# Four gate rows sent through DRAM instead of the matrix engine, and a written order for the last in-products

## The chip, the cores and the metric

The program runs on one core of a Trainium2 chip. The metric is the device time of one execution in microseconds. The core has a matrix engine (TensorE, PE in the profile; PEld is its weight load, which overlaps the matmuls), three engines for elementwise work (VectorE = DVE, ScalarE = ACT, GpSimd = POOL) and a queue of DMAs that SyncE (SP) issues. On-chip memory is SBUF, with 128 partitions; matmuls write to PSUM, whose banks the kernel gives out from two pools.

## What is computed

A two-layer diffusion backbone over 512 latent tokens and 256 context tokens of width 1024. The first layer mixes tokens by pooling, the second by attention; each is followed by a squared-ReLU MLP of width 4096. Six rows of 1024 numbers for each layer, made from a conditioning vector, shift, scale and gate the sub-layers:

```python
for i in range(DEPTH):
    sh1, sc1, gt1, sh2, sc2, gt2 = ada_mods(c, w_ada[i], b_ada[i])
    csh1, csc1, cgt1, csh2, csc2, cgt2 = ada_mods(c_ctx, w_ada[i], b_ada[i])
    ...
    x = x + gt1 * rms_norm(y_lat, g_mix_post[i])
    m_lat = sq_relu_mlp(modulate(rms_norm(x, g_mlp_pre[i]), sh2, sc2), w_mlp_in[i], w_mlp_out[i])
    x = x + gt2 * rms_norm(m_lat, g_mlp_post[i])
    if not last:
        ...
        ctx = ctx + cgt2 * rms_norm(m_ctx, g_mlp_post[i])
```

The change is about the gates (gt1, gt2, cgt2): rows of 1024 numbers by which every token's row is multiplied, so that on the chip each of the 128 partitions, one for a token, wants a copy of the whole row.

## The kernel before, in words

Activations and weights are 32-bit. A product of two of them is made from three matmuls of rounded parts: each operand is split into a high part (cast on ACT, POOL) and a low part (the difference, mostly on DVE).

**Stages.** Pooling mixer; first MLP over all 768 tokens in six rows of 128 (0 to 3 latent, 4 and 5 context); projection to q, k and v; attention; output projection; second MLP over the four latent rows; output. Each MLP runs over sixteen groups of 256 hidden columns.

**First MLP.** The hidden columns of one group are seven in-products over half the tokens each (class `Seven`, chains 0 to 6, in a Strassen-like scheme; tiles psin in PSUM), combined by ACT and DVE into the hidden rows, which are squared and split into high and low (rb). Then each of the six token rows takes twelve matmuls for each half of its 1024 columns (tiles pso, `out_mm`), which are added to acc (`out_ev`). The last two groups are done together in `finish`: each row takes 24 pso matmuls a half, ordered so that the ones that need only the older group come first. `finish` goes through the rows in the order 4, 5, 0, 1, 2, 3. Rows 4 and 5 are added to acc by DVE; the others start from a copy of acc in PSUM (ACT, pso<-acc).

**After a row.** ACT squares and sums it (junk, ss), POOL or DVE makes the inverse root rs, DVE multiplies the row by the gate (work<-acc,gate or work<-pso,gate) and adds it, scaled, to the residual (xr or xl). Normed rows are transposed by PE (psx<-ident,acc), modulated by ACT and DVE (acc<-psx) and split (ra), as operands of the projection (psq). The tiles pso, psx's neighbours psg, psq and psy share a pool of four PSUM banks (psB): a new one can only start when the row product of an old one has read it.

**Gates before.** `gate_cols` makes a gate as eight columns of 128 (tile gc), one value to a partition. To repeat it over partitions there are two ways. `gate_rows` lets PE multiply a broadcast column by the identity, eight matmuls (in the program; each shows as two in the trace) of 128x128, and ACT copies the two halves from PSUM. `gate_diag` splits gc into high and low (gh), lets DVE make two diagonal tiles of 128x1024 (diag), sums them with two matmuls a half by a matrix of ones (psg<-diag,onesr), and again ACT copies. Before the change, the two GT2 gates of layer 0 are made by `gate_diag` in `before0`, which is called between the last in-products and `finish(0)`; the GT2 gate of layer 1 by `gate_diag` within `finish(1)`; the GT1 gate of layer 1 by `gate_rows` near the end of attention. Tile gate holds two rows (ci 0 for latent, 1 for context tokens).

**What sets the order.** Python code hands operations over in the order of written times (`Steps`, `at(time, function)`), which is their priority; a scheduler that simulates engines then sets each engine's order from it. Within an engine, instructions run in that order. Some are pinned to the program's order (`pin`), and some get a manual dependency (`tc.add_manual_dep(.., ISSUE)`), which only orders them on their own engine, without a semaphore. DMAs stand in SP's order; one that waits holds those behind it.

## Time and profile before

| what | value |
|---|---|
| median of three runs | 1156.81 us (1156.76 to 1157.1) |
| the profiled execution | 1157.33 us |
| its span in the profile | 1155.2 us, clock 0.999 |
| PE busy | 1134.3 us (98%) |
| PEld, DVE, ACT, POOL busy | 979.8, 938.0, 644.8, 74.4 us |
| chain that ended last | PE 94%, DMA 3%, ACT 2%, DVE 1% |
| psg<-diag matmuls | 12, 3.7 us |
| psg<-ident matmuls | 48, 6.2 us (16 of them at the end of attention) |
| diag products on DVE | 6, 7.2 us |
| gate<-psg copies on ACT | 12, 6.6 us |

The span runs from the first to the last instruction of the profiled execution; the execution's own time has about 2 us around it. A row of the trace gives a start and a length in us from the span's start; matmuls are pipelined, so that neighbouring rows overlap a little, and twelve matmuls of 128x512 take about 2.75 us from one start to the next.

### The profile page before, as it was taken

Reading aid. Unit: us, or ns where it says so; the run is one execution under the profiler, and the core shown is the slowest. Engines: PE = TensorE matmul, PEld = TensorE weight load, DVE = VectorE, ACT = ScalarE, POOL = GpSimd, SP = SyncE. Lnnn points to the kernel's source line nnn. Section 1 sums busy time; section 2 is a strip of 40 time slices with the busy share of each in tenths; the row PEclk is TensorE's granted clock in tenths of the full one; section 3 lists DMA queues with packets and bytes.
Section 4 is the critical chain, followed back from the end, with each engine's and each line's share of the span. In section 5 each row is a group of like instructions: output and inputs, shape, how many; then the busy total and the mean of one; then the engine's idle time right before and its main releaser. Section 6 shows DMA issues by size and latency. Waiting matters only on the chain.

```text
span 1155.2 us, 15680 instructions
## 1 busy us (share of the span) xinstructions
PE 1134.3 (98%) x6026; PEld 979.8 (85%) x6026; DVE 938.0 (81%) x1551; ACT 644.8 (56%) x1150; POOL 74.4 (6%) x82
## 2 busy tenths in 40 slices
PE   6999999999999999999999999999999999999998
PEld 5579889998899988998888889988988888888886
DVE  5798488889989898998778698978887779778876
ACT  6476655555435434555786378863876436534524
POOL 3040000000000000000231312100000000000000
PEclk9999999999999999999999999999999999999999
DMA  9992233244434444344442200145244224314303
GB/s 355 398 390 99 74 109 110 80 140 146 146 109 146 146 147 146 109 146 146 187 142 99 84 1 20 34 134 208 82 146 146 79 68 146 109 40 144 109 28 118
DMA packets 95305, 152.08 MB, mean 132 GB/s; under 512 B 2896, under 2 KB 68224, under 8 KB 95232
## 3 DMA queue, kind: packets, MB, share of 16 engines
q1 hardware_dynamic: 95136, 151.07, 37.8%
q8 instruction: 47, 0.77, 0.3%
q14 instruction: 26, 0.21, 0.1%
q10 hardware_dynamic: 96, 0.02, 0.0%
HBM read 141.65 MB, written 9.44 MB: 131 GB/s over the span
## 4 chain that ended last, share of the span: by engine, by line
PE 94%; DMA 3%; ACT 2%; DVE 1%; issue 0%; POOL 0%; DVEq 0%; SPq 0%; ACTq 0%
PE pso L68 36%; PE psin L68 35%; PE psq L68 7%; PE psy L68 4%; PE po L68 3%; PE pss L68 3%; DMA raw<-in_w_ada 2%; PE pspt L68 1%; PE psada L68 1%; PE pspool L68 1%; PE psx L68 1%; PE psg L68 1%; ACT ra L68 0%; DMA xr<-in_ctx 0%; DMA gate<-in_band 0%; ACT xr L68 0%
## 5 line engine op out<-in xcount | busy, mean ns | idle before, releaser
L68 PE MATMUL pso<-units,rb 128*128 128x512 f32 x1152 | 277.3, 392 | 0.0
L68 PEld LDWEIGHTS pso<-units,rb 128*128 128x128 f32 x1152 | 214.9, 188 | 41.7
L68 DVE TENSOR_TENSOR acc<-acc,pso 128x512 f32<-128x512 f32 x192 | 128.3, 680 | 61.5 <-PE pso L68 61.4
L68 DVE SCALAR_TENSOR_TENSOR rows<-raw,cond,rows 128x256 f32<-128x256 f32 x280 | 123.4, 483 | 0.9
L68 PE MATMUL psin<-ra 128*128 128x512 f32 (+1 forms) x424 | 112.4, 369 | 0.6 <-ACT work L68 0.6
L68 PE MATMUL psin<-ra,rb 128*128 128x512 f32 (+1 forms) x384 | 101.6, 360 | 0.0
L68 DVE TENSOR_TENSOR units<-raw,units 128x1024 fp32r<-128x1024 f32 (+2 forms) x69 | 82.4, 1203 | 13.8 <-ACT units L68 13.7
L68 ACT CAST units<-raw 128x1024 fp32r<-128x1024 f32 (+2 forms) x71 | 70.7, 1019 | 41.0 <-PE pso L68 21.8
L68 PE MATMUL psin<-rb,ra 128*128 128x384 f32 (+1 forms) x324 | 90.6, 356 | 0.0
L68 PEld LDWEIGHTS psin<-ra 128*128 128x128 f32 x424 | 77.8, 188 | 12.3 <-ACT work L68 1.0
L68 ACT ACTIVATE work<-psin 128x512 f32<-128x512 f32 (+3 forms) x66 | 36.0, 551 | 84.6 <-PE psin L68 82.4
L68 PE MATMUL psin<-ra,units 128*128 128x384 f32 x432 | 82.6, 336 | 0.4 <-ACT psin L68 0.4
L68 PE MATMUL pso<-units,pairs 128*128 128x512 f32 x336 | 82.3, 389 | 0.0
L68 PEld LDWEIGHTS psin<-ra,units 128*128 128x128 f32 x432 | 76.4, 188 | 3.2 <-ACT psin L68 0.5
L68 PEld LDWEIGHTS psin<-ra,rb 128*128 128x128 f32 x384 | 66.7, 189 | 11.5 <-issue 0.8
L68 PEld LDWEIGHTS pso<-units,pairs 128*128 128x128 f32 x336 | 63.1, 188 | 13.1
L68 PE MATMUL psin<-sums,units 128*128 128x384 f32 x336 | 63.6, 336 | 0.0
L68 PEld LDWEIGHTS psin<-rb,ra 128*128 128x128 f32 x324 | 58.6, 188 | 5.5
L68 ACT COPY acc<-pso 128x512 f32<-128x512 f32 x68 | 38.5, 592 | 40.1 <-PE pso L68 39.9
L68 PEld LDWEIGHTS psin<-sums,units 128*128 128x128 f32 x336 | 59.0, 188 | 1.3
L68 ACT CAST rb<-raw 128x2048 fp32r<-128x2048 f32 (+2 forms) x18 | 25.8, 1431 | 58.3 <-PE pso L68 55.8
L68 ACT ACTIVATE work<-work 128x768 f32<-128x768 f32 (+1 forms) x50 | 41.4, 831 | 28.8 <-DVE work L68 28.3
(226 smaller groups left out, 2118.9 us busy)
## 6 DMA issues: line engine op xcount, KB each, us to landing
raw<-in_w_ada SPq DMA_DIRECT2D x48, 1024.0 KB, 5.4
raw<-in_w_mlp_in SPq DMA_DIRECT2D x32, 1024.0 KB, 5.3
raw<-in_w_mlp_out SPq DMA_DIRECT2D x32, 1024.0 KB, 6.0
raw<-in_w_qkv SPq DMA_DIRECT2D x6, 1024.0 KB, 5.1
spill<-xl SPq DMA_DIRECT2D x8, 512.0 KB, 5.5
xl<-spill SPq DMA_DIRECT2D x8, 512.0 KB, 7.1
raw<-in_w_o SPq DMA_DIRECT2D x4, 1024.0 KB, 5.0
xl<-in_x SPq DMA_DIRECT2D x4, 512.0 KB, 5.5
```

Source lines behind the costliest of these rows:

```text
L68: z = made(*args, **kw)
```

## The change

A tensor grows of four rows is added in DRAM. `gate_away` makes the columns gc and stores them there as one row of 1024 numbers (a DMA of 128 x 8 single elements on SP's queue); `gate_back` loads that row into gate for all 128 partitions (one DMA, 512 KB written). The three `gate_diag` calls and the one `gate_rows` call go. The stores of layer 0's GT2 gates are called in groups 7 and 8 of the first MLP, that of layer 1's GT1 in `before0` (the scheduler moves it up to the middle of the first MLP, as its columns are ready there), and that of layer 1's GT2 in the second MLP; the loads are called where the gates were made before, ahead of the loads of the residual. On SP the stores stand between loads of weights (two between the loads that were issued at 291.79 and 304.17 before), the first two loads directly ahead of xr<-spill and xl<-spill.

Beside that, in `finish(0)` the matmuls of the first two rows (4 and 5) get manual dependencies: of row 4, matmuls n = 0 and 1 of each half are free, n = 2 and 3 come behind the last matmul of chain 4, and the rest of row 4 and all of row 5 behind chain 6.

```diff
--- before.py
+++ after.py
@@ -113,6 +113,7 @@
     psA = ctx.enter_context(tc.tile_pool(name="psA", bufs=2, space=PSUM))
     psB = ctx.enter_context(tc.tile_pool(name="psB", bufs=4, space=PSUM))
     spill = ctx.enter_context(tc.tile_pool(name="spill", bufs=1, space=bass.MemoryType.DRAM)).tile([P, NT, D], F32, name="spill")
+    rows_out = ctx.enter_context(tc.tile_pool(name="grows", bufs=1, space=bass.MemoryType.DRAM)).tile([4, D], F32, name="grows")
 
     acc = const.tile([P, NT * D], F32, name="acc")
     ident = const.tile([P, P], F32, name="ident")
@@ -379,6 +380,16 @@
                               start=True, stop=True)
                 pin(z, i == 0 and m == GT1)
             sc.copy(gate[:, ci, 512 * h:512 * h + 512], ps)
+
+    row_of = {(0, GT2, 0): 0, (0, GT2, 1): 1, (1, GT1, 0): 2, (1, GT2, 0): 3}
+
+    def gate_away(i, m, ci):
+        gc = gate_cols(i, m, ci)
+        with nc.allow_non_contiguous_dma(reason="one column of gates for each partition"):
+            sy.dma_start(rows_out[row_of[i, m, ci]].rearrange("(k p) -> p k", p=P), gc)
+
+    def gate_back(i, m, ci):
+        sy.dma_start(gate[:, ci, :], rows_out[row_of[i, m, ci]].partition_broadcast(P))
 
     def gate_diag(i, m, ci, to=None):
         to = ci if to is None else to
@@ -853,7 +864,7 @@
 
     class Seven:
         def __init__(self, products, hid):
-            self.products = products
+            self.products, self.ends = products, {}
             self.a, self.ntok = (hH, hL), TOK
             self.hid = [z.rearrange("p (f n) -> p f n", n=TOK) for z in hid]
 
@@ -861,8 +872,8 @@
             (wH, wL), (aH, aL) = self.products[n]
             for k in range(4):
                 for m, (w, a) in enumerate(((wH, aH), (wH, aL), (wL, aH))):
-                    te.matmul(bank, w[k], a[k], start=start and k == 0 and m == 0, stop=stop and k == 3 and m == 2,
-                              skip_group_check=True)
+                    self.ends[n] = te.matmul(bank, w[k], a[k], start=start and k == 0 and m == 0,
+                                             stop=stop and k == 3 and m == 2, skip_group_check=True)
 
         def run(self, between=None):
             px, py = (psA.tile([P, 2, 512], F32, tag="a", name="psin") for _ in range(2))
@@ -1025,6 +1036,8 @@
 
     pso = {}
 
+    order0, behind_chains = [], []
+
     def out_mm(i, parts, t, cols=HALVES):
         at_ = place_of[t] if i == 0 else t
         ts_ = slice(at_ * P, (at_ + 1) * P)
@@ -1039,13 +1052,19 @@
                 sc.copy(ps[:, 0:w], accv[:, t, c0:c0 + w])
         seq = [(a, f, w) for (_, (hi, lo), (wH, wL)) in parts for f in range(2)
                for a, w in ((hi, wH), (hi, wL), (lo, wH))]
+        order_ = order0
         order = [(n, h) for n in range(len(seq)) for h in range(len(cols))]
         if len(parts) > 1:
             order.sort(key=lambda z: (z[0] >= (9 if cols == HALVES else 0), z[1]))
         for n, h in order:
             a, f, w = seq[n]
-            te.matmul(pss[h][:, 0:cols[h][1]], a[:, f, ts_], w[:, f, cols[h][0]:sum(cols[h])],
-                      start=(n == 0 and not seeded[t]), stop=(n == len(seq) - 1), skip_group_check=seeded[t])
+            z = te.matmul(pss[h][:, 0:cols[h][1]], a[:, f, ts_], w[:, f, cols[h][0]:sum(cols[h])],
+                          start=(n == 0 and not seeded[t]), stop=(n == len(seq) - 1), skip_group_check=seeded[t])
+            if len(parts) > 1 and behind_chains and t in order_[0:2]:
+                lead = t == order_[0] and n < 4
+                if t == order_[0] and n < 2:
+                    continue
+                tc.add_manual_dep(z.ins, behind_chains[0 if lead else 1].ins.name, ISSUE, reason="row order")
         pso[t] = pss
 
     def out_ev(i, parts, t, cols=HALVES):
@@ -1096,7 +1115,10 @@
                     out_mm(0, [part], t)
                     out_ev(0, [part], t)
         before_last()
+        order0.extend(order)
+        behind_chains.extend(inner.ends[z] for z in (4, 6))
         finish(0, [part, (NG - 1, inner.hid, wo_)], order, last)
+        del behind_chains[:]
 
     def mlp1(inner, last):
         nonlocal xr, gate, junk
@@ -1199,6 +1221,8 @@
             inner = inner_of(2 * p + 2)
             if p == 1:
                 ada_fin(1, GT2, parts[1], 1)
+            if p == 3:
+                gate_away(1, GT2, 0)
         whole = lambda n: tuple(z.rearrange("p (f n) -> p f n", f=2) for z in (home[n], home[n + 1]))
         half_ = lambda n: (home[n][:, 0:1024], home[n][:, 1024:2048])
         wo_ = []
@@ -1225,9 +1249,10 @@
                 add(m7_, m7_, m5)
         closing.close()
         xr, gate, junk = residents(ctx)
+        gate_back(1, GT2, 0)
         for t in range(NL):
             sy.dma_start(xr[:, t], spill[:, t])
-        finish(1, [(NG - 2 + q, last_[q].hid, wo_[q]) for q in range(2)], range(NL), last, ((5.1, gate_diag, 1, GT2, 0),))
+        finish(1, [(NG - 2 + q, last_[q].hid, wo_[q]) for q in range(2)], range(NL), last, )
 
     dual = [(0, GT2, 2), (1, SC1, 2), (1, SH1, 2)]
     lone = [(1, m, 1) for m in (GT1, SC2, SH2)]
@@ -1260,6 +1285,8 @@
             pinned[0] = False
         if g == 4:
             head_gains()
+        if g in (7, 8):
+            gate_away(0, GT2, g - 7)
         if g > 1:
             ada_step()
         if g == 2:
@@ -1450,10 +1477,11 @@
         nonlocal xr, gate, junk
         for u in due:
             ada_fin(*u[1:])
+        gate_away(1, GT1, 0)
         S["held"].close()
         xr, gate, junk = residents(held[1])
-        gate_diag(0, GT2, 0)
-        gate_diag(0, GT2, 1)
+        gate_back(0, GT2, 1)
+        gate_back(0, GT2, 0)
         for t in (4, 5, 0, 1, 2, 3):
             sy.dma_start(xr[:, t], spill[:, t])
         qring.append(Ring([unit[0], unit[2], unit[1]]))
@@ -1619,7 +1647,7 @@
         at(39.192, lambda: split(*raws[3], False, False, False, 1))
         at(39.193, lambda: split(*raws[3], False, False, False, 2))
         at(45.691, lambda: split(*raws[3], False, False, False, 3))
-        at(39.281, gate_diag if False else gate_rows, 1, GT1, 0)
+        at(36.95, gate_back, 1, GT1, 0)
 
     def output(st, base):
         at = lambda i, fn, *args: st.at(base + i, fn, *args)
```

Three places in the order of the instructions follow. The first is PE's queue at the end of the first MLP: psin are the last in-products (chains 3, 5, 4 and 6 in the order of execution, chain 4 being the rows with sums), psada a small sum for the modulation, pso the rows of `finish(0)`. Before:

```order
L68 MATMUL psg<-diag,onesr 128x512 x2
L68 MATMUL psin<-sums,ra 128x384
L68 MATMUL psin<-rb,ra 128x384
L68 MATMUL psin<-sums,ra 128x384 x2
L68 MATMUL psin<-rb,ra 128x384
L68 MATMUL psin<-sums,ra 128x384 x7
L68 MATMUL psg<-diag,onesr 128x512 x2
L68 MATMUL psin<-ra 128x384 x12
L68 MATMUL psg<-diag,onesr 128x512 x2
L68 MATMUL pso<-units,rb 128x512 x12
L68 MATMUL psg<-diag,onesr 128x512 x2
L68 MATMUL pso<-units,rb 128x512 x84
```

With the change, from the psada rows on:

```order
L68 MATMUL psada<-parts,sel 32x8 x4
L68 MATMUL pso<-units,rb 128x512 x4
L68 MATMUL psin<-ra,units 128x384 x12
L68 MATMUL psin<-rb,ra 128x384 x12
L68 MATMUL psin<-sums,ra 128x384
L68 MATMUL psin<-rb,ra 128x384
L68 MATMUL psin<-sums,ra 128x384 x2
L68 MATMUL psin<-rb,ra 128x384
L68 MATMUL psin<-sums,ra 128x384 x7
L68 MATMUL pso<-units,rb 128x512 x4
L68 MATMUL psin<-ra 128x384 x12
L68 MATMUL pso<-units,rb 128x512 x100
```

The four pairs of psg are gone; four pso of row 4 now stand ahead of chain 3 and four more ahead of chain 6, and 100 follow chain 6 at once. Up to the first psx that makes 4 + 4 + 100 = 108 pso, where 12 + 84 = 96 stood; twelve fewer follow it.

The second is DVE's queue some 25 us later, where rows 1 and 2 of `finish(0)` are gated (work<-pso,gate; the first pair is row 1, the next single one the first half of row 2), context rows are modulated (acc<-psx) and split (ra), and a weight is split (units<-raw). Before:

```order
L68 TENSOR_TENSOR work<-pso,gate 128x512 x2
L68 SCALAR_TENSOR_TENSOR xl<-work,rs,xl 128x1024
L68 TENSOR_SCALAR acc<-psx,avec_100,mods_97 128x256 x6
L68 TENSOR_TENSOR ra<-acc,ra 128x2x256
L68 TENSOR_TENSOR work<-pso,gate 128x512
L68 TENSOR_TENSOR ra<-acc,ra 128x2x256 x2
L68 TENSOR_TENSOR work<-pso,gate 128x512
L68 TENSOR_TENSOR units<-raw,units 128x512
```

With the change:

```order
L68 TENSOR_TENSOR work<-pso,gate 128x512 x2
L68 TENSOR_SCALAR acc<-psx,avec_103,mods_100 128x256 x3
L68 SCALAR_TENSOR_TENSOR xl<-work,rs,xl 128x1024
L68 TENSOR_SCALAR acc<-psx,avec_103,mods_100 128x256 x3
L68 TENSOR_TENSOR ra<-acc,ra 128x2x256 x3
L68 TENSOR_TENSOR units<-raw,units 128x512
L68 TENSOR_TENSOR work<-pso,gate 128x512
L68 TENSOR_TENSOR ra<-acc,ra 128x2x256
L68 TENSOR_TENSOR work<-pso,gate 128x512 x2
```

Ahead of the first half of row 2 there now stand three ra and the units split, where one ra stood; and the residual xl comes between the two halves of the modulation.

The third is PE's queue at the end of attention: po are the last products with v, psg the row gate, psy the output projection.

```order
 L68 MATMUL pspt<-ident,acc 128x128 x6
 L68 MATMUL po<-units,rb 128x256 x29
-L68 MATMUL psg<-ident,gc 128x128
+L68 MATMUL psy<-lent,ra 128x512
 L68 MATMUL po<-units,rb 128x256 x7
-L68 MATMUL psg<-ident,gc 128x128 x7
-L68 MATMUL psy<-lent,ra 128x512 x12
+L68 MATMUL psy<-lent,ra 128x512 x11
 L68 MATMUL psy<-ra 128x512 x12
 L68 MATMUL psy<-lent,ra 128x512 x12
```

The sixteen matmuls of the gate (two for each instruction here) leave, and one matmul of the output projection stands among the last po.

## The prediction

> **What bounds the kernel now.** I read three views, in this order: busy time by stretch, the chain of work that ended last, and the rows in time order at the places of the change. First the stretches: start and end, length, then busy time and instruction count of PE, PEld, DVE, ACT and POOL, the granted clock, the DMA share and GB/s.
>
> ```profile
> 90.00:540.00 450.00, 450.00 (x2297) 406.41 (x2297) 385.47 (x698) 231.46 (x344) 0.00 (x0) 1.00 0.37 122
> 540.00:580.00 40.00, 39.60 (x204) 33.81 (x203) 27.66 (x30) 27.23 (x56) 8.99 (x7) 1.00 0.55 201
> 580.00:690.00 110.00, 109.11 (x547) 91.16 (x546) 86.26 (x154) 70.17 (x194) 28.39 (x37) 1.00 0.24 82
> ...
> 770.00:830.00 60.00, 59.41 (x344) 51.89 (x343) 46.87 (x91) 29.20 (x70) 1.90 (x1) 1.00 0.46 158
> 830.00:1130.00 300.00, 300.00 (x1331) 248.21 (x1331) 236.65 (x273) 152.43 (x195) 0.00 (x0) 1.00 0.31 105
> ```
>
> From 90 us on, PE pauses for less than 1 us in any of these stretches, at a clock of 1.00. So **a matmul that goes gives back its own time and a new wait of PE is paid in full**, while work that goes from DVE or ACT gives nothing by itself: it counts only where PE waits for it.
>
> **Term A, the end of the first MLP: -2.4 us.** The chain there (start, length, what, count), and the PE row with the idle time ahead of it:
>
> ```profile
> 543.25 4.45 PE psin L68 x24
> 547.70 0.46 PE psg L68 x2
> 548.16 2.11 PE psin L68 x12
> 550.27 0.04 issue
> 550.30 0.73 PE psg L68 x2
> 551.03 2.26 PE psin L68 x12
> 553.29 0.46 PE psg L68 x2
> 553.75 2.73 PE pso L68 x12
> 556.48 0.46 PE psg L68 x2
> 556.94 19.09 PE pso L68 x84
> ```
>
> ```profile
> 543.25 2.37 PE L68 MATMUL psin<-ra,units 128*128 128x384 f32 x12 [0.37 <-ACT psin L68]
> ```
>
> The four psg pieces are the two removed diagonal gates: 0.46 + 0.73 + 0.46 + 0.46 = 2.11 us. In the 0.73 hides a wait of about 0.3 us, since chain 6 needs a DVE sum of the matmuls just ended; four pso matmuls (a quarter of a us each) now stand in that place, so work that is to be done anyway covers the wait. Four more stand ahead of chain 3 and cover its 0.37 us. That makes 2.11 + 0.37 = 2.48, and I take 2.4. What is late next are the last hidden rows, which ACT makes out of chain 6:
>
> ```profile
> 554.54 0.84 ACT L68 ACTIVATE work<-work 128x768 f32<-128x768 f32 x1
> 555.41 0.84 ACT L68 CAST rb<-work 128x768 fp32r<-128x768 f32 x1
> ```
>
> From the end of chain 6 to their end, 556.25, that took 556.25 - 553.29 = 3.0 us. The new order wants the first of them 16 pso after chain 6, at 19.09/84 = 0.227 us each after 3.6 us, so 0.6 us is left.
>
> **Term B, from the last rows to the first projection: +2.2 us, a new wait.** The chain here, and DVE's rows in the same time:
>
> ```profile
> 581.74 1.53 PE psx L68 x14
> 583.27 5.48 PE pso L68 x24
> 588.75 0.11 PE psx L68
> 588.86 3.66 PE psq L68 x16
> ```
>
> ```profile
> 582.96 1.29 DVE L68 SCALAR_TENSOR_TENSOR xl<-work,rs,xl 128x1024 f32<-128x1024 f32 x1 [1.69 <-POOL rs L68]
> 584.16 2.80 DVE L68 TENSOR_SCALAR acc<-psx,avec,mods 128x256 f32<-128x256 f32 x6
> 586.88 0.99 DVE L68 TENSOR_TENSOR ra<-acc,ra 128x512 fp32r<-128x512 f32 x1
> 587.79 0.68 DVE L68 TENSOR_TENSOR work<-pso,gate 128x512 f32<-128x512 f32 x1
> 588.39 1.80 DVE L68 TENSOR_TENSOR ra<-acc,ra 128x512 fp32r<-128x512 f32 x2
> ```
>
> The first psq needs a PSUM bank in which a finished pso row lies; the DVE product work<-pso,gate frees it. Before, this ended at 588.47, just ahead of the psq at 588.6. In the new order two further ra<-acc,ra and one units<-raw,units stand ahead of that product on DVE, and DVE takes its rows in order. Count from T, the end of the fourteen psx (583.27 before). PE needs the bank after 24 pso and two psx, at T + 5.48 + 0.22 = T + 5.7. DVE has, from T on: three acc<-psx (half of 2.80), xl (1.29), three acc<-psx (1.40), three ra (0.99 + 1.80), one units, one product (0.68). The units row and the two ends of the shape 128x512 stand here:
>
> ```profile
> 591.17 1.32 DVE L68 TENSOR_TENSOR units<-raw,units 128x512 fp32r<-128x512 f32 x1
> ```
>
> ```profile
> 1123.12 0.69 DVE L68 TENSOR_TENSOR units<-work,units 128x512 fp32r<-128x512 f32 x1 [0.61 <-ACT units L68]
> ```
>
> With the slow durations the sum is 8.9, so PE waits 8.9 - 5.7 = 3.2 us; with 0.69 for each of the four 128x512 rows it is 7.5 and the wait 1.8. Neighbouring rows overlap by nearly 0.1 each, which takes 0.5 to 0.8 off both: the ends are about 1.2 and 2.7. I take 2.2, nearer the upper end, because POOL splits weights in the same stretch before and after. The queue behind the product holds the second half of the row and the next row's two; psq matmuls want those banks one by one, 12 matmuls (about 2.8 us) apart, so they come out in time once the first wait is paid.
>
> Which durations hold there is a question on which the Trainium skill has a rule: its page GPSIMD Engine Reference, § 1. Specifications, says that the SBUF interface is shared with VectorE, with contention when a DVE instruction has two SBUF inputs. The two units rows above (1.32 beside POOL, 0.69 with POOL idle) agree. By that rule the fast end would hold from the moment POOL is done; by the rows of this stretch the slow one; the sum would be -3.8 or -2.3.
>
> **Term C, the end of attention: -1.7 us.** Again the chain:
>
> ```profile
> 766.49 0.22 PE psg L68 x2
> 766.72 0.83 PE po L68 x7
> 767.55 1.56 PE psg L68 x14
> ```
>
> The sixteen psg of the row gate go: 1.78 us, of which I take 1.7. One psy now stands among the last po, and the rest follow directly. The first psy group needs at its last three matmuls a cast pair that ACT and DVE make of a po that ended shortly before; I leave 0.08 us for that.
>
> **Term D, the end of the second MLP: -0.9 us.**
>
> ```profile
> 1132.01 0.93 PE psg L68 x4
> ```
>
> The last diagonal gate costs 0.93 us of PE; the pso that follow it have their operands long before.
>
> **The DMAs: 0.** Loads around the gate stores, and the first use of a gate:
>
> ```profile
> 291.79 0.37 SPq L146 DMA_DIRECT2D raw<-in_w_mlp_out  x1
> 304.17 0.37 SPq L146 DMA_DIRECT2D raw<-in_w_mlp_in  x1
> ```
>
> ```profile
> 562.16 1.29 DVE L68 TENSOR_TENSOR work<-acc,gate 128x512 f32<-128x512 f32 x2
> ```
>
> ```profile
> spill<-xl SPq DMA_DIRECT2D x8, 512.0 KB, 5.5
> xl<-spill SPq DMA_DIRECT2D x8, 512.0 KB, 7.1
> ```
>
> ```profile
> grow<-in_g_k SPq DMA_DIRECT2D x1, 64.0 KB, 11.1
> ```
>
> The two gate stores of layer 0 are issued between those two loads, where SP has 304.17 - 291.79 = 12 us with nothing to issue; the others stand in gaps as wide. SP waits for gc, which DVE makes at once, so nothing behind it is held. No row shows a store in pieces of four bytes; the nearest (spill<-xl, large pieces) lands in 5.5 us and keeps no later load back. Its price lies between 0 and a load that is late. The returning rows are 512 KB each, as those of xl<-spill are; the first two are issued at chain 4's end (550.27) and used from 562 on, 12 us for a landing of about 7, so 0 again. A broadcast row, grow<-in_g_k, took 11.1 in the crowded start, which would just do. The other two return long before their use. If this cover were gone, DVE would stand in work<-acc,gate and PE soon after.
>
> **Sum:** -2.4 + 2.2 - 1.7 - 0.9 = -2.8 us. The profiled execution took 1157.33 us, so it would take 1154.5; the median of the runs is 1156.81, half a us lower, which gives **1154.0 us**.
>
> **Rivals.**
> *No wait in B.* If DVE is ahead of its rows by more than I think, or ACT's casts come earlier, the product is out by T + 5.7. For it: ACT also has one seed copy and the gate copies less. Against: the sum of DVE rows, which exceeds 5.7 even with every row fast. Time: 1156.8 - 5.0 = 1151.8. Chance 0.2.
> *The order gives back all.* B at 2.7, and two or three more waits of 0.3 to 0.8 us at psq and pk, where ACT and DVE now follow a new order as well (580 to 690 has 0.9 us of idle PE already): -5.0 + 2.7 + 1.5 = -0.8, so 1156.0. Chance 0.15.
> *Slower, by the returning gate.* The two gate loads stand ahead of xr and xl on SP. If a row read 128 times over lands in 20 us instead of 6, the DVE product of 562.16 waits until 570, and with it, in order, the acc<-acc,pso behind it that frees the banks of row 5: PE loses the 8 us, less 3 that I allow for banks still free, so -2.8 + 5 = +2.2, 1159. It decides from a landing of some 17 us. Against it: the rows of 512 KB. Chance 0.1.
> *Slower, by the stores.* The Trainium skill's page DMA: Bandwidth & Descriptors, § Rules for kernel authors, says that a non-contiguous last dim lowers to one descriptor per element, and § Specifications puts the smallest efficient transfer at 512 B. Here one gate store is 1024 elements. As a mechanism of this kernel: two stores that hold the queue longer than the 12 us gap make the weight load at 304.17 late. At 10 us each they would cost PE 8 us less the several us by which that load now precedes its use; 1158 to 1159. The gaps speak against it. Chance 0.05. From the same page, § Bandwidth, 10.5 ns a packet would make 64 pieces an engine 0.7 us, an estimate by which nothing would be late; no run here shows it.
>
> **How the numbers follow.** A measurement of this kernel tells about 0.2% (2.3 us, here 1154.5) from no change. The forecast has 0.5; its own range is 1153.2 to 1155.2 (B from 1.4 to 3.2), two thirds of it under 1154.5. Faster: 0.35 + 0.2 = 0.55; within: 0.15 + 0.15 = 0.30; slower: 0.15. For 8 in 10 the range reaches down to the case without a wait and up past the one that gives all back: 1151.3 to 1157.0.
>
> **What would show it.** No psg<-diag after 290 us and no psg<-ident after 100 us; chain 3 of the last in-products without idle time ahead of it; one PE idle of 1.2 to 2.7 us ahead of the first psq after the last pso, released by DVE work; psy directly behind po; the tail at unchanged length after the last pso. Wrong: no such idle time at psq, PE idle ahead of weights at 310 us, or DVE's work<-acc,gate released by a DMA.

## The result, and the profile after

The changed kernel took **1167.18 us** (median of 5 runs, 1166.5 to 1168.29), the kernel before 1156.95 in the same comparison (5 runs, 1156.76 to 1157.14): a ratio of 1.009 with the 95% interval [1.0075, 1.0105]. It is 10 us slower, where 3 us faster was forecast. The profiled execution took 1167.72 us with a span of 1165.9, against 1157.33 and 1155.2 before.

Busy time by stretch of the kernel after (start and end, length, then busy time and instruction count of PE, PEld, DVE, ACT and POOL, granted clock, DMA share, GB/s):

```profile
90.00:540.00 450.00, 449.37 (x2273) 402.68 (x2273) 380.86 (x687) 228.43 (x341) 0.00 (x0) 1.00 0.37 120
...
580.00:700.00 120.00, 115.34 (x557) 95.41 (x556) 87.37 (x153) 73.31 (x201) 30.71 (x39) 0.97 0.25 86
...
840.00:1140.00 300.00, 300.00 (x1320) 246.15 (x1319) 234.44 (x268) 151.27 (x193) 0.00 (x0) 1.00 0.31 103
```

In the first and the last of these stretches PE is as busy as before, but for 0.63 us, at a clock of 1.00, and yet fits fewer matmuls into the same time: 2273 against 2297 in the first 450 us, 1320 against 1331 in the 300 us near the end. So two things are to be found: a loss with no idle time, spread over both MLPs, and one from 580 to 700 us, where PE is idle for 4.7 us and the clock falls.

The first stands in the groups of the page. Before, then after (busy us in all, mean ns of one, then the idle time ahead):

```profile
L68 PE MATMUL pso<-units,rb 128*128 128x512 f32 x1152 | 277.3, 392 | 0.0
...
L68 PE MATMUL psin<-ra,units 128*128 128x384 f32 x432 | 82.6, 336 | 0.4 <-ACT psin L68 0.4
L68 PE MATMUL pso<-units,pairs 128*128 128x512 f32 x336 | 82.3, 389 | 0.0
...
L68 PE MATMUL psin<-sums,units 128*128 128x384 f32 x336 | 63.6, 336 | 0.0
```

```profile
L68 PE MATMUL pso<-units,rb 128*128 128x512 f32 x1152 | 282.0, 395 | 0.0
...
L68 PE MATMUL pso<-units,pairs 128*128 128x512 f32 x336 | 84.1, 394 | 0.0
L68 PE MATMUL psin<-ra,units 128*128 128x384 f32 x432 | 83.1, 338 | 0.0
...
L68 PE MATMUL psin<-sums,units 128*128 128x384 f32 x336 | 64.4, 339 | 0.6 <-ACT psin L68 0.6
```

Same matmuls, same count, same clock: these four groups take 7.8 us longer (4.7 + 1.8 + 0.5 + 0.8). All four read units. The start-to-start time of pso<-units,rb between 100 and 280 us, averaged over the trace's records, is 0.2294 us before and 0.2329 after. Three nanoseconds are easily taken for noise; over 1488 pso they are not.

The second is the place of term B. PE's rows in time order (start, length, idle time ahead of it and what ended it), then DVE's:

```profile
584.59 1.69 PE L68 MATMUL psx<-ident,acc 128*128 128x128 f32 x14
586.04 5.83 PE L68 MATMUL pso<-units,rb 128*128 128x512 f32 x24
591.71 0.38 PE L68 MATMUL psx<-ident,acc 128*128 128x128 f32 x2
595.88 5.49 PE L68 MATMUL psq<-rb,ra 128*128 128x512 f32 x12 [3.79 <-DVE work L68]
601.16 3.20 PE L68 MATMUL psq<-units,ra 128*128 128x512 f32 x12
```

```profile
586.32 1.45 DVE L68 TENSOR_SCALAR acc<-psx,avec,mods 128x256 f32<-128x256 f32 x3 [1.90 <-PE psx L68]
587.69 1.28 DVE L68 SCALAR_TENSOR_TENSOR xl<-work,rs,xl 128x1024 f32<-128x1024 f32 x1
588.88 1.44 DVE L68 TENSOR_SCALAR acc<-psx,avec,mods 128x256 f32<-128x256 f32 x3
590.24 4.38 DVE L68 TENSOR_TENSOR ra<-acc,ra 128x512 fp32r<-128x512 f32 x3
594.54 0.68 DVE L68 TENSOR_TENSOR units<-raw,units 128x512 fp32r<-128x512 f32 x1
595.15 0.68 DVE L68 TENSOR_TENSOR work<-pso,gate 128x512 f32<-128x512 f32 x1
595.75 0.67 DVE L68 TENSOR_TENSOR ra<-acc,ra 128x512 fp32r<-128x512 f32 x1
```

The wait is there, at the instruction and with the releaser that were named. It is longer than forecast: 3.79 us. And it has a tail: the twelve psq behind it take 5.49 us. Short stretches around it show why (columns as above; the clock is the number after POOL):

```profile
590.00:595.80 5.80, 2.09 (x11) 1.44 (x9) 5.80 (x7) 5.39 (x16) 5.64 (x6) 0.92 0.50 166
595.80:599.50 3.70, 3.62 (x9) 2.85 (x10) 3.61 (x6) 2.12 (x7) 0.55 (x1) 0.50 0.94 319
599.50:602.80 3.30, 3.30 (x11) 2.59 (x10) 1.28 (x1) 2.41 (x7) 0.55 (x1) 0.67 1.17 339
602.80:606.00 3.20, 3.20 (x20) 2.70 (x18) 0.42 (x1) 1.60 (x3) 0.00 (x0) 1.00 0.64 259
```

TensorE's clock was halved for 6.83 us, from 594.85 to 601.68. The first 1.03 us of that PE was still idle; the other 5.8 us of work at half clock cost 2.9 us more than at full clock. So B cost about 6.7 us, not 2.2.

Third, the stores. Issues of the gate rows (KB each, median us to landing), and ACT's cast of the weight whose load was issued 9 us behind the third store (335.77 against 326.78):

```profile
gate<-grows SPq DMA_DIRECT2D x4, 512.0 KB, 5.7
...
grows<-gc SPq DMA_DIRECT2D x4, 4.0 KB, 13.3
```

```profile
344.20 1.05 ACT L68 CAST units<-raw 128x1024 fp32r<-128x1024 f32 x1 [5.13 <-DMA raw<-in_w_mlp_in]
```

```profile
355.83 2.38 PE L68 MATMUL psin<-sums,units 128*128 128x384 f32 x12 [0.63 <-ACT psin L68]
```

A store of 4 KB landed in 13.3 us; the weight load of 1 MB behind the third one took 8.4 us (5.3 before), and PE waited 0.63 us some 12 us later, where before it did not.

### The profile page after: what moved, and what is told of

Read it like the earlier page. It is cut to its first block, busy times and chain, and to the rows that moved or that the text cites. A ratio compares the mean times of both kernels' runs of the same rounds, so it can differ in the third digit from the quotient of the medians.

```text
span 1165.9 us, 15604 instructions
## 1 busy us (share of the span) xinstructions
PE 1140.6 (98%) x5998; PEld 978.1 (84%) x5998; DVE 926.2 (79%) x1539; ACT 641.4 (55%) x1142; POOL 75.9 (7%) x82
## 5 line engine op out<-in xcount | busy, mean ns | idle before, releaser
L68 PE MATMUL pso<-units,rb 128*128 128x512 f32 x1152 | 282.0, 395 | 0.0
## 6 DMA issues: line engine op xcount, KB each, us to landing
xl<-spill SPq DMA_DIRECT2D x8, 512.0 KB, 10.5
```

What stands on the lines that cost most here:

```text
L68: z = made(*args, **kw)
```

## The experiments

### Where units lies

**Theory 1:** the diagonal gates had two small tiles named gh (64 bytes a partition each). With their code they are gone, and every tile allocated behind them, the ring of raw and units above all, lies 128 bytes lower in each partition: units at byte 124704 instead of 124832 (the places are those in the built program). PE reads units more slowly there. **Rivals:** the new order alone makes PE slower; or DMA traffic does. The edit changes no instruction and no order of after, and gives the 128 bytes back:

```diff
     spill = ctx.enter_context(tc.tile_pool(name="spill", bufs=1, space=bass.MemoryType.DRAM)).tile([P, NT, D], F32, name="spill")
+    small.tile([P, 32], F32, tag="pad", name="pad", bufs=1)
```

The second kernel has 16 words there instead of 32, which puts units at 124768.

> The changed kernel with 128 unused bytes put back ahead of the tile units, so that units lies where it lay before the change (the two gh tiles that went were 128 bytes); the order of all instructions is that of the changed kernel. Theory (address): a pso matmul takes 0.227 us again from start to start instead of 0.232, about 7.5 us in all; the time is 1167.2 - 7.5 = 1159.7 us, and the wait ahead of the first psq stays at 3 to 4 us. Rival (the pace is of the chip, the program's code or the stores, not of the address): 1167 us and 0.232.

> The same with 64 unused bytes. If only the place of units matters and the rule is a grid of 128 bytes or more, pso keeps 0.232 us or takes another value between 0.226 and 0.235; if only the former place is good by itself, 0.232. If the address has nothing to do with it, 0.232 here and in the run with 128 bytes alike.

With 128 bytes: **1159.94 us** (7 runs, ratio to before 1.0026 [1.0015, 1.0037]), so 7.2 us came back without any change of an instruction. With 64 bytes: 1165.6 (one run), with the group at 282.0 us and 395 ns, as in the changed kernel. With 128 bytes:

```profile
L68 PE MATMUL pso<-units,rb 128*128 128x512 f32 x1152 | 277.9, 392 | 0.6 <-ACT pso L68 0.4
```

The theory also has to make the kernel before slow. There one gh tile instead of two moves units to 124768:

```diff
-        gh = small.tile([P, 2, KT], F32R, tag="gh", name="gh", bufs=2)
+        gh = small.tile([P, 2, KT], F32R, tag="gh", name="gh", bufs=1)
```

> The kernel before, with one gh buffer instead of two, so that units lies 64 bytes lower; PE's order is the same but for one pair of matmuls, DVE's differs a little about the diagonal gates. Theory (address): 0.232 to 0.233 us for a pso matmul, as with 64 bytes in e2_pad64, 5.5 to 7.5 us more than before: 1162.5 to 1164.5. Rival (the pace hangs on the changed program in another way): 1157.

```profile
L68 PE MATMUL pso<-units,rb 128*128 128x512 f32 x1152 | 281.5, 395 | 0.0
```

It took **1163.53 us** (5 runs, 1.0057 [1.0044, 1.0069]): 6.4 us slower than before, with no gate store, no new order at the end of the MLP and no wait at psq (the order of the small gh rows on DVE moved, PE's almost not). That rules out both rivals as the cause of the slower pso.

What about the place counts? Two more kernels of after: one moves rb and ra up by 128 bytes and so puts units back at 124832 while its distance to rb stays that of after (32 unused words in the pool of constants); one puts units at 124800 (24 unused words ahead of it).

> The kernel after with 128 unused bytes per partition in the pool of constants, ahead of every tile that lies for the whole run (ra, rb, units and the rest all move by 128 bytes); instructions and order are those of after. units then stands at byte 124832 of its partition, as in the kernel before, but its distance to rb and ra is the one of after. If what counts is where units itself stands: one pso starts every 0.2295 us, and the time is 1159 to 1161. If what counts is its distance to rb: 0.2329 us, and 1166 to 1168.

> The kernel after with 96 unused bytes per partition ahead of units alone, so that it stands at byte 124800, between the places 124768 (slow, two runs) and 124832 (fast, three runs); rb stands as in after. If the pace changes with distance step by step, one pso starts every 0.230 to 0.232 us and the time is 1161 to 1165; if only one place is fast, 0.2329 us and 1165 to 1168; if the rule is a border that lies below 124800, 0.2295 us and 1159 to 1161.

Both took long, 1168.5 and 1168.49 (one run each, before 1157.62 on that chip), half a us above the longest time expected. Rows of the first, and behind them pso<-ra,pairs as it stands in the changed kernel:

```profile
L68 PE MATMUL pso<-units,rb 128*128 128x512 f32 x1152 | 281.7, 395 | 0.4 <-ACT pso L68 0.4
...
L68 PE MATMUL pso<-units,pairs 128*128 128x512 f32 x336 | 83.0, 391 | 0.0
...
L68 PE MATMUL pso<-ra,pairs 128*128 128x512 f32 x168 | 40.3, 395 | 0.0
...
L68 PE MATMUL psin<-rb,ra 128*128 128x512 f32 x128 | 49.9, 389 | 0.0
```

```profile
L68 PE MATMUL pso<-ra,pairs 128*128 128x512 f32 x168 | 39.2, 389 | 0.0
```

The same units at their old place are read slowly together with rb, which has moved, while with pairs, which has not, most of the loss is gone (391 ns; 389 before, 394 after). The third row shows the same without units: ra has moved with rb, pairs has not, and pso<-ra,pairs went from 389 ns, which it takes in before and after alike, to 395. So neither the place of units by itself sets the pace, nor anything else that belongs to units; where a matmul's two operands lie relative to each other fits. Fast was the distance units - rb of 45568 bytes, which is 89 x 512; slow were 45440, 45504 and 45536. The distances of the tile pairs (at byte 159648) with 389 ns are multiples of 512 as well: 68 x 512 to units, 253 x 512 to ra. A multiple of 128 isn't enough (45440 is 355 x 128), and 32 bytes beside the fast place cost as much as 128.

Is it the distance, or each operand's own place within 512 bytes (416 for all these tiles when fast)? The kernel with 128 bytes among the constants moved rb and ra together, to place 32, and psin<-rb,ra in the last of its rows stayed at 389 ns, as in before and after. That speaks for the distance; no run moved these two apart. Still open: what in the chip does it, and whether a multiple of 256 would do.

### The wait at the first psq

**Theory 2:** the wait and the half clock both come from row 2's product standing behind three ra and a units on DVE, and ACT's sum of squares of that row behind three casts. **Rival:** with the wait gone, ACT and the casts for psq make the next wait as long. The edit (on top of the 128 bytes) writes three dependencies that hold only the order: row 2's first half ahead of the casts on ACT, its product ahead of the later ra and of the units row on DVE:

```diff
+            z = mean_square(src, ss, n, root and n == len(cols) - 1)
+            if t == 2 and n == 0 and highs:
+                for b in highs:
+                    tc.add_manual_dep(b.ins, z.ins.name, ISSUE, reason="row order")
...
+            z = gated(t, yg[t], src, c0, c0 + w, pool)
+            if t == 2 and c0 == 0 and lows:
+                for b in lows[1:]:
+                    tc.add_manual_dep(b.ins, z.ins.name, ISSUE, reason="row order")
```

> With the 128 bytes, and written dependencies that put ACT's square sum and DVE's product of row 2's first half ahead of the splits of the context rows and of the weight split. Theory (the wait ahead of psq comes from DVE's order, and the half clock behind it from the length of that wait): the wait falls from 3.8 to under 1.5 us, no stretch of half clock follows, and the time is 3.8 + 2.7 - 1 = 5.5 us below the run with 128 bytes alone, about 1154. Rival (the half clock comes of something else there, or another wait takes its place): only 2 to 3 us less, about 1157.

It took **1155.38 us** (11 runs, 0.9986 [0.9978, 0.9995]), 4.6 less than with the 128 bytes alone (5.5 were expected). PE's rows, and a stretch of them:

```profile
589.10 0.70 PE L68 MATMUL psq<-rb,ra 128*128 128x512 f32 x2 [0.31 <-DVE work L68]
590.62 3.00 PE L68 MATMUL psq<-rb,ra 128*128 128x512 f32 x10 [0.82 <-DVE ra L68]
```

```profile
592.00:600.00 8.00, 7.86 (x42) 6.47 (x41) 7.13 (x11) 6.41 (x20) 3.01 (x3) 1.00 0.92 267
```

1.1 us of waiting is left, in two pieces, and the clock stays at 1.00. With the order on DVE alone (where the units row is held behind the product itself, not behind the last ra):

> As e3_first_row, but with the written dependencies on DVE alone: ACT's order stays that of the changed kernel, where row 2's square sum comes behind the casts. DVE's product is then out at about 7.1 us after the psx, where PE arrives at 5.7: a wait of 1.4 to 2.4 us ahead of the first psq. If the half clock needs a wait of about 3.8 us, as the runs so far have it, none follows and the time is 1156 to 1157.5; if a wait of 2 us is enough, 2 us or more are added, 1158 or more.

```profile
590.61 2.14 PE L68 MATMUL psq<-rb,ra 128*128 128x512 f32 x8 [1.29 <-DVE work L68]
593.39 1.20 PE L68 MATMUL psq<-rb,ra 128*128 128x512 f32 x4 [0.64 <-DVE ra L68]
```

1156.33 us (one run, within the spread of the eleven above, 1154.97 to 1156.65). The waits are 1.93 us in all, 0.8 more than with both orders: about that is what ACT's order is worth here, and DVE's is worth the rest. A wait of 1.3 us does not halve the clock either. In the profiles of all seven kernels with a wait of 3.75 to 3.92 us it was halved, in two for 6.83 us, in five for 3.41.

What tells the two apart is where the wait falls. In each trace the changes of the clock inside the kernel lie whole multiples of 3.413 us apart (171, 2 and 165 of them in after), as if it were set once in each such period. In the two kernels it fell 1 us before the wait had ended (594.85 against 595.88 in after, 592.70 against 593.75 with the 128 bytes), so that this period still began with 1 us of idle time, and a second period at half clock followed. In the other five it fell between 0.3 us before the end of the wait and 1.5 us behind it, and one period was all. The Trainium skill's page TensorE: Matmul & The Clock Gate, § What's actually happening, has this rule: after about one window of 3.4 us without work the array drops to half its clock, and takes about one window of work to get back; the window runs freely. This case agrees, with half clock behind 3.75 us and none behind 1.29; no run lies between. But no such window had to be idle as a whole: of the 3.78 us of wait in the kernel with 64 bytes, 1.87 lay in one period of 3.413 us and 1.91 in the next.

The seven times of the kernel with the 128 bytes lie at 1159.4 to 1159.9 and at 1161.0 to 1161.6. One period at half clock more or less (1.7 us of work) would do that; it is not shown, since of the others only the mean clock is on record.

### The stores

**Theory 3:** the stores keep the DMA engines for 10 to 15 us, as a thousand separate elements, and slow what runs beside them on any queue. **Rival:** only the queue is blocked. Issued on ACT's queue (with the 128 bytes):

```diff
-            sy.dma_start(rows_out[row_of[i, m, ci]].rearrange("(k p) -> p k", p=P), gc)
+            nc.scalar.dma_start(rows_out[row_of[i, m, ci]].rearrange("(k p) -> p k", p=P), gc)
```

> With the 128 bytes, and the four gate stores issued from ACT's queue instead of SP's. If a store of single elements holds only the queue it stands in, the loads of w_mlp_in behind it land in 5.3 us again (7.0 and 8.4 in the changed kernel) and the wait of 0.6 us at 355 us goes: 0.6 us less than with 128 bytes alone. If it occupies the DMA engines whatever the queue, they land in 7 to 8.5 us as before. ACT's order in the second MLP moves a little as well.

1159.2 us (one run), and the two weight loads beside the stores still landed in 7.4 and 9.0 us: the rival falls. The packets of after say where the time is not: the 1056 of the third store all started between 330.42 and 331.25 us and took 9 ns each, yet the store landed at 340.03. From 335.8 to 340.0, with the store and the next weight load under way, the core's DMA moved 16 GB/s, from 340.0 to 344.2 it moved 234. What holds the engines meanwhile, no packet shows. Next, the kernel of the written order with the gates transposed on PE first, so that the store has eight pieces of 512 bytes:

```diff
+        te.transpose(ps[0:KT, 0:P], gc, ident)
+        sc.copy(flat[0:KT, 0:P], ps[0:KT, 0:P])
+        sy.dma_start(rows_out[row_of[i, m, ci]].rearrange("(k p) -> k p", p=P), flat[0:KT, 0:P])
```

> The kernel of e3_first_row, with the gate stored as eight pieces of 512 bytes: PE transposes the columns (one matmul of 128 x 8 for each gate), ACT copies the result, and the store goes from there. Theory (the 1024 single elements keep the DMA engines busy and make the next weight load late): the stores land in under 4 us instead of 13, both loads of w_mlp_in in about 5.3, the waits of PE at 319 to 356 us go (1.6 us in e3_first_row), and the time is 1.5 to 2.5 us below e3_first_row, about 1153. Rival (the waits come of the order of ACT and DVE in groups 7 to 9): they stay, 1155.4. The new PE and ACT work moves the order within the MLPs a little.

Two loads issued 3.5 and 2.7 us behind such a store (which now stand at 318.56 and 351.49) landed in 5.1 and 5.25 us, so the size or the number of the pieces fits. That is weaker than it looks: the landing of these stores is not in the trace, and the load at 304.00, which landed in 5.3, has no store ahead of it any more. The time did not follow: **1157.18** (11 runs, 1.0001 [0.9992, 1.001]), a miss. With the transposes the first MLP was written in another order, with new waits, as one of 0.68 us for ACT ahead of a pso at 443.64. PE's idle time from 290 to 546 us was 1.40 us, hardly less than the 1.55 with row 2 first, and the way to the first psq took 0.8 us longer; what makes up the rest of the 1.8 us is not shown.

So the stores were left as they are and only issued behind the weight load that they had stood ahead of, by one more dependency each:

```diff
+            if (i, m, ci) in late_of:
+                tc.add_manual_dep(z.ins, late_of[i, m, ci].ins.name, ISSUE, reason="row order")
```

> The kernel of e3_first_row, with the three stores in the first MLP written behind the load of w_mlp_in that they stood ahead of; no other engine's order changes. Theory (a store of single elements slows the weight load issued after it, and PE waits for that load's casts): both loads land in about 5.3 us again, PE's idle time from 290 to 546 us falls from 1.55 to under 0.4 us, and the time is 1 to 2.5 us below e3_first_row: 1153 to 1154.4. Rival (the waits belong to the new order of ACT and DVE in groups 7 to 9, or the loads of w_ada that are now behind the stores bring waits of their own): 1155 to 1156.

**1154.13 us** (8 runs, 0.9979 [0.9967, 0.999]): the fastest version seen, and faster than the kernel before. SP's issues there:

```profile
304.30 0.37 SPq L150 DMA_DIRECT2D raw<-in_w_mlp_in  x1
304.72 0.58 SPq L395 DMA_DIRECT2D grows<-gc  x1
```

That weight landed in 5.7 us, against 8.0 in the kernel without this edit, and PE's idle time from 290 to 546 us fell from 1.55 to 0.76, where under 0.4 was expected. The delay moved in part: the w_ada load issued at 311.03, now behind the store, took 11.8 us instead of about 5, and the 0.76 us are the wait at 353.5 that was there without the edit; the cast ahead of it began 6.8 us after its weight's load was issued (8.7 without the edit, 5.3 before). The intervals of the two kernels overlap, so the gain of 1.2 us is not shown by the times alone.

### The parts of the change by themselves

Both kernels keep the diagonal gates' tiles, so units stays at 124832. One has the last two gates (terms C and D) in the new form, the other the first two with the written order (term A):

```diff
+        gate_away(1, GT1, 0)
...
+            if p == 3:
+                gate_away(1, GT2, 0)
...
+        gate_back(1, GT2, 0)
...
+        at(36.95, gate_back, 1, GT1, 0)
```

```diff
+        if g in (7, 8):
+            gate_away(0, GT2, g - 7)
...
-        gate_diag(0, GT2, 0)
-        gate_diag(0, GT2, 1)
+        gate_back(0, GT2, 1)
+        gate_back(0, GT2, 0)
```

> Only two of the four gates go through DRAM: layer 1's GT1 and GT2; layer 0's are made by diagonals as before, and there is no written order. gh stays, and units keeps its place. Terms C and D of the prediction alone: -1.7 - 0.9 = -2.6 us if the one store in the first MLP costs nothing, 1154.5; with a late weight load of up to 1 us about 1155.5. If C and D gave nothing, 1157.

> The other two alone, with the written order; gh stays, and units keeps its place. Term A gives -2.4, the wait ahead of psq and the half clock behind it cost 3.8 + 2.7 (or 1.5, where the half clock ends sooner), the stores 1 to 2: 1157 + 4 to 6 = 1161 to 1163. If the wait came of the whole change and not of these two gates, 1155.

The first took **1157.23 us** (11 runs, 1.0001 [0.9992, 1.001]), a miss by 2.7 us. C and D came in full (141.21 and 22.02 us in the columns of the table below), but the first MLP, which neither gate touches, was written in another order and lost 3 us, 1.6 of it in new waits such as this:

```profile
444.58 2.03 PE L68 MATMUL psin<-ra,units 128*128 128x384 f32 x10 [0.63 <-DVE units L68]
```

The second took 1160.74 (one run), with 3.92 us of waiting at the first psq and 3.4 us of half clock. Cutting PE's records at the same instructions gives each kernel by stages (us; worked out from the start times in the traces):

| | first psin to first psq | psq | to the last psy | second MLP's psin | from there to the last pso |
|---|---|---|---|---|---|
| before | 515.10 | 83.22 | 143.04 | 311.31 | 23.00 |
| after | 522.30 | 86.44 | 141.61 | 313.79 | 22.34 |
| after + 128 bytes | 520.21 | 85.64 | 141.23 | 311.31 | 22.02 |
| + row 2 first | 515.67 | 84.05 | 141.24 | 311.31 | 22.02 |
| + stores later | 514.17 | 84.07 | 141.24 | 311.29 | 22.02 |
| first two gates alone | 517.29 | 84.38 | 142.96 | 311.27 | 22.97 |

Read across the columns: the third shows C (143.04 to 141.24), the fifth D (23.00 to 22.02), the fourth the place of units and nothing else (313.79 against 311.31); the first two hold A, B and the stores.

## Why the prediction was wrong, step by step

**What bounds the kernel: right.** PE is without a gap in most stretches, so each matmul's own duration counts in full. The prediction used this for matmuls that go, and not for the thousands that stay.

**The step that failed most is not one of the terms but the assumption under their sum:** that every matmul which the change doesn't touch keeps its duration. The sum takes its terms off the execution of before ("The profiled execution took 1157.33 us, so it would take 1154.5"), and no line asks what the removed code had allocated. Two tiles went with it, the operands moved, and that cost 6.4 us by the kernel before with one gh tile, 7.2 by after with and without the 128 bytes. No rival had it either.

**Term B: the mechanism right, the size wrong.** "I take 2.2", between 1.2 and 2.7; it was 3.79. Counted from T (586.28 here), DVE's rows up to the product lasted as forecast within 0.1 us, except two: the three ra took 4.38 us instead of 0.99 + 1.80, and units 0.68 instead of 1.32. POOL split weights beside some of the ra rows that the estimate was taken from, and beside all three here:

```profile
587.71 3.67 POOL L68 TENSOR_TENSOR units<-raw,units 128x512 fp32r<-128x512 f32 x2 [1.63 <-ACT units L68]
591.34 1.07 POOL L68 CAST units<-raw 128x512 fp32r<-128x512 f32 x1
592.37 1.70 POOL L68 TENSOR_TENSOR units<-raw,units 128x512 fp32r<-128x512 f32 x1
```

The three took 1.69, 1.09 and 1.75 us; at 595.75, with POOL done, one takes 0.67. The prediction priced such rows at one slow or one fast duration. They have neither: each of the three ended 0.55 us after the POOL instruction that ran when it began (at 591.93, 592.95 and 594.62, after 591.38, 592.40 and 594.07). So did two of the three ra rows of before that the estimate used (0.99 us, ending at 587.87 after 587.32; 1.20 us, at 589.59 after 589.04). All 35 ra and units rows of this shape that began beside a split or cast on POOL, in the traces of all these kernels, ended so, within 0.01 us. The product work<-pso,gate, which reads one operand from PSUM, took 0.68 to 0.69 beside them. So the price of such a row is what is left of POOL's instruction, and the new order met POOL earlier in its work.

Then the half clock, which no step had: a wait of 1.29 us did not bring it, one of 3.79 did, for another 2.9 us; no run shows whether the forecast 2.2 would have.

**Term A: came, and a part was lost elsewhere.** Rows of PE before, in time order, behind the chains that the prediction shows, and then of after from chain 3 on:

```profile
553.12 0.62 PE L68 MATMUL psg<-diag,onesr 128*128 128x512 f32 x2
553.58 2.89 PE L68 MATMUL pso<-units,rb 128*128 128x512 f32 x12
556.32 0.62 PE L68 MATMUL psg<-diag,onesr 128*128 128x512 f32 x2
556.77 3.61 PE L68 MATMUL pso<-units,rb 128*128 128x512 f32 x15
```

```profile
548.97 2.27 PE L68 MATMUL psin<-ra,units 128*128 128x384 f32 x12
...
555.24 1.10 PE L68 MATMUL pso<-units,rb 128*128 128x512 f32 x4
556.18 2.24 PE L68 MATMUL psin<-ra 128*128 128x384 f32 x12
558.26 2.03 PE L68 MATMUL pso<-units,rb 128*128 128x512 f32 x8
```

Before, from the start of the 0.37 us of idle time ahead of chain 3 (542.88) to 556.77 are 13.89 us, 11.15 without the twelve pso in between (553.58 to 556.32). After, from 548.97 to 558.26 are 9.29 us, 8.35 without the four pso (555.24 to 556.18); chain 3 started without a wait. That is -2.8, where -2.4 was forecast. But the kernel with the first two gates alone gained only 1.5 us up to the first psq (517.29 - 515.10 = 2.19, less 3.92 of waiting there, and its other idle time is 0.2 shorter): about 1 us went in the new order of the first MLP, at no wait that a row shows.

**Terms C and D: right.** -1.8 against -1.7, -1.0 against -0.9, in every kernel that has them and reads units at full pace. No psg row is left there.

**The DMAs, "0": wrong by a little, and right about the returning gate.** gate<-grows landed in 5.7 us and nothing waited for it, so that rival falls. The rival of the stores, given 0.05, is the one that showed, though small, and not by holding its queue. The 12 us gap was no cover, since a store in flight slows the load beside it. The packets of the page, before and after:

```profile
DMA packets 95305, 152.08 MB, mean 132 GB/s; under 512 B 2896, under 2 KB 68224, under 8 KB 95232
```

```profile
DMA packets 100042, 154.20 MB, mean 132 GB/s; under 512 B 7120, under 2 KB 72448, under 8 KB 99968
```

4224 more are under 512 bytes, some 1056 for each of four stores: one for every element, as the rule says that the prediction cited from the Trainium skill's page DMA: Bandwidth & Descriptors, § Rules for kernel authors. The 0.7 us that the prediction worked out from the same page's § Bandwidth, at 10.5 ns a packet, fits the packets themselves (9 ns each, all of the third store's begun within 0.83 us). What failed was to read from it that nothing would be late: the landing, with a median of 13.3 us, took 19 times as long. The cost to PE was 0.63 us of waiting here. In the kernels that read units at full pace and have all four stores PE's idle time from 290 to 546 us was 1.4 to 2.4 us, and 0.17 with the first two stores alone: the third, issued at 326.78 here, is the one that hurts. That the slower PE hides a part of it in after would fit, but is not shown.

**The sum.** Place of units +6.4, wait 3.8 and half clock 2.9, stores 0.3 (0.63 of idle time against 0.37), A -2.8, C -1.8, D -1.0 make +7.8; the spans differ by 10.7. Some 2.9 us stay unassigned: the rows of the four groups would put up to 7.8 on the place, and about 1 us lies in the new order of the first MLP. With the three unforeseen costs undone, the change gives 1154.13, within 0.2 us of the forecast, in part by chance: 1.1 us of waiting at psq stands there for the 2.2 of term B, and 1 us in the first MLP that the forecast did not have.

## What to carry to other kernels

When a change removes or adds a tile, compare the addresses of all the others before reading anything else into the time, and look for matmuls of one group whose mean has moved by 1%: where PE is never idle, that is the whole loss. A forecast wait near 3 us on TensorE has two prices, one with the clock kept and one with it halved, and belongs in the range with both: here 1.3 us cost no clock and 3.75 did. A row on DVE with two inputs in SBUF that shares its time with POOL is to be priced by what POOL will be doing when it starts, not by the length that it had elsewhere. And an edit to a scheduled kernel moves instructions hundreds of us away from it; a part tried alone is only as good as the check that the rest kept its order.

## What the runs showed of the hardware that was not expected

- A matmul's pace depends on where its two SBUF operands lie: 0.2294 us for one pso with units and rb 45568 bytes (89 x 512) apart, 0.2329 in after, 128 bytes less, and mean records of 395 ns instead of 392 at 32, 64 and 128 bytes less; 6.4 us over this kernel.
- After 3.75 to 3.92 us without work TensorE ran at half clock, for one or two periods of 3.413 us by where the wait fell among them; after 1.3 us it did not.
- A DVE row of 128x512 with both inputs in SBUF (ra, units) that began beside a weight split or cast on POOL ended 0.55 us after that instruction's end, in all 35 cases here: 0.69 to 1.77 us long, by how much of POOL's instruction was left, against 0.67 alone.
- A store of 1024 single elements (4 KB) landed in 10 to 15 us, though its packets took 9 ns each, and took a 1 MB load behind it from 5.3 to between 7.0 and 9.6 us, on its own queue or another's. Behind stores in pieces of 512 bytes two such loads took 5.1 and 5.25.
